# Two more features of a squared-ReLU MLP as seven half-size products: a blind prediction and its test

## The chip, the cores and the metric

The kernel runs on one core of a Trainium2 chip. The metric is the device time of one execution in microseconds (us); lower is better. Before the change the median of three runs is 1310.76 us (1310.34 to 1311.7).

## What is computed

The reference is an encoder trunk of two layers on a sequence of 512 rows of 1024 numbers: a mixer (layer 1 a gated delta rule, "GDN", layer 2 a gated linear attention, "GLA"), each followed by an MLP. The change is in the MLP, and in a constant that GLA uses.

```
def _sq_relu_mlp(h, w1, w2):
    a = jax.nn.relu(jnp.matmul(h, w1))
    return jnp.matmul(a * a, w2)
...
    x = _layernorm(DEEPNORM_ALPHA * x + _sq_relu_mlp(x, mlp_w1[i], mlp_w2[i]).astype(x.dtype), ln2_g[i], ln2_b[i])
```

w1 is 1024x4096 and w2 4096x1024, in float32. A float32 product is made of three matmuls: each operand is split in a high and a low part (a cast on ScalarE, L102, and a subtraction on VectorE, L107), and high x high, high x low and low x high are added up in PSUM (`mm3`, L128 to L130).

## The kernel before, in words

An MLP (`mlp`, from L352 on) works in four groups of 1024 hidden units, eight features of 128 units each. First the features of group 0 are made. Then, group by group, the second matmul of a group (`second`) is interleaved with the first matmul of the next group (`stream`): half chunks of six and chunks of twelve 512-column matmuls for w2 (tiles pX, pY, pZ) alternate with products for w1. The last group's second matmul (`last`) stands alone.

How a feature is made. In group 0 all eight are full products (`feature`): 24 matmuls of 512 columns into one PSUM bank (tile pj), then relu and square on ScalarE (L383, L384). In the other groups two features at a time (`Pair`) are made by seven half-size products after Strassen and Winograd, each of 12 matmuls of 256 columns: 84 for two features. They are numbered 1, 2, 6, 5, 7, 3, 4 in the order in which TensorE makes them. `prepare` and `late` make the weights: a split (L102, L107) for products 1 and 2 together, sums on VectorE (L464), half a split for product 5 (L470, L471), a split for 6 and 4, and one for 7 and 3. `x_blocks` makes the combinations of x once per MLP (L433 to L442) and splits them.

Three accumulators of 256 columns take the products: X (1, 6, 7, 4), Z (2) and Y (5, 3). A PSUM bank holds two. X has a bank of its own (tile fx), Z and Y share one (fyz). Between products the accumulators are read: X by ScalarE after product 1 (L499) and after 6 (L506), Z by VectorE after 2 (L503), Y by ScalarE after 5 (L509), X by VectorE after 7 (L513), Y after 3 (L517), X by ScalarE after 4 (L523, then L524). In the stream products 1 and 2 follow each other without a chunk between them; so do 6 and 5, and 7 and 3. A pair ahead has its weights made while the pair before it is multiplied.

What sets the order. A scheduler orders each engine's instructions; within `in_order(PE)` TensorE keeps the order in which the code is written. VectorE, ScalarE and GpSimd each work through their own list in order. Buffers: three for raw weights (wst), three for split weights (wh and wl), eight for raw w2 (w2r), two PSUM banks for the first matmul's products (tag pj). Each group also adds quarters of w2 to each other by accumulating transfers that GpSimd issues (L415).

`sel_masks` (L785) makes eight masks of 128x128 for GLA on GpSimd, by memsets, affine selects, subtractions and casts (L792 to L805); they are called in the first MLP through `extra`, and stand in GpSimd's list ahead of the first accumulating transfer.

Of the kernel before, what the change touches and what calls it, by code (L numbers as in the profile page):

```python
# [8 lines left out]
F32 = mybir.dt.float32  # L9
# [342 lines left out]
def mlp(c, w1, w2, g, b, out=None, extra=None, room=0):  # L352
# [14 lines left out]
    with c.banks(pj=2, X=2, Y=2, Z=2), tc.tile_pool(name="mlp", bufs=2) as pool:  # L367
# [82 lines left out]
        class Pair:  # L450
# [10 lines left out]
            def prepare(self):  # L461

                (t0, t1), h = self.t, KT // 2
                plus = lambda a, b: V.tensor_tensor(a, a, b, ALU.add)  # L464
# [26 lines left out]
            def products(self, h):  # L491

                f = 2 * self.p
                h0, h1 = [h[f // HF][:, (f + j) % HF, :] for j in range(2)]
                l, r = slice(0, HT), slice(HT, S)
                x, yz = c.bank([P, 2, HT], F32, name="fx", tag="pj"), c.bank([P, 2, HT], F32, name="fyz", tag="pj")
                X, Z, Y = x[:, 0, :], yz[:, 0, :], yz[:, 1, :]
                self.mm(X, 1)
                A.copy(h0[:, l], X)  # L499
                yield  # L500
                self.mm(Z, 2)
                with tc.high_priority(offset=200):
                    V.tensor_tensor(h0[:, l], h0[:, l], Z, ALU.add)  # L503
# [19 lines left out]
                A.activation(h0[:, r], X, AF.Relu)  # L523
                A.activation(h0, h0, AF.Square)  # L524
                yield
# [4 lines left out]
        def pair(src, where="ah"):  # L530
            return c.split(src, [P, HF, HT], pool=ring(where))
# [9 lines left out]
        def quarters(h):  # L541
            return [h[j][:, :, HT * i:HT * i + HT] for i in range(2) for j in range(2)]
# [155 lines left out]
                full(2 + j, 0, X[j])  # L698
            return norm, second_normed

        todo = [(gi, p) for gi in range(1, G) for p in range(GF // 2)]
        ready = {}

        def begin(i):

            if i < len(todo):
                ready[i] = Pair(*todo[i])
# [14 lines left out]
            act(ps, h[0][:, f, :])  # L722
        xa = {}
        xb = x_blocks(xa)
        for f in range(4, GF):
            feature(0, f, h)
            if f >= 5:
                next(xb)
            if f == 4:
                load(0, 0, 0)  # L730
            if f == 5:
                load(0, 0, 1)
            if f == 6:
                load(0, 1, 1)
                with tc.issue_after(c.last_hi.ins), tc.issue_after(c.last_lo.ins):
                    split(1)
                a = pair(quarters(h)[0])
        begin(0)
        prepare(0)
        finish(0)  # L740
        if extra:
            extra(lambda: pool.tile([P, P], F32, name="tmp", tag="tmp", bufs=2))
        def stream(gi, nh):

            for p in range(GF // 2):
                i = (gi - 1) * (GF // 2) + p
                for n, _ in enumerate(ready[i].products(nh)):
                    if n == 0:
                        begin(i + 1)
                    elif n == 1:  # L750
                        ready[i].late(1, (7, 3))
                    elif n == 3:
                        prepare(i + 1)
                    elif n == 5:
                        finish(i + 1)
                    if p == 3 and n == 2 and gi + 1 == G:
                        load(gi, 1, 0, c.wst)
                    if p == 3 and n == 2:
                        split(1, None if gi + 1 < G else True)
                        stream.a = pair(quarters(nh)[0])  # L760
                    yield

        for gi in range(G - 1):
            nh = new_h()
            more = stream(gi + 1, nh)
            n, k = 28, 0
            m = 24 if gi + 2 == G else 28
            with c.in_order(mybir.EngineType.PE):
                for i, _ in enumerate(second(gi, h, a)):
                    upto = n if i + 1 == m else min(i + 2, 7 * (i // 7) + 7) if i % 7 in (0, 2, 4, 6) else k  # L770
                    while k < upto:
                        next(more, None)
                        k += 1
                for _ in more:
                    pass
            h, a = nh, stream.a
        with c.in_order(mybir.EngineType.PE):
            norm, normed = last(G - 1, h, a)
# [5 lines left out]

def sel_masks(c, pool, tmp):  # L785

    nc = c.nc
    out = {}
    prev = None
    for w in (1, 2, 4, 8, 16, 32, 64, 128):  # L790
        f = tmp().rearrange("p (a b) -> p a b", b=w)
        nc.gpsimd.memset(f, 1.0)  # L792
        if w < P:
            nc.gpsimd.affine_select(out=f, in_=f, compare_op=ALU.is_ge, fill=0.0, base=0,
                                    pattern=[[-w, P // w], [0, w]], channel_multiplier=1)
            nc.gpsimd.affine_select(out=f, in_=f, compare_op=ALU.is_ge, fill=0.0, base=w - 1,
                                    pattern=[[w, P // w], [0, w]], channel_multiplier=-1)
        fl = f.rearrange("p a b -> p (a b)")
        if w != 2:
            m = pool.tile([P, P], mybir.dt.uint8, name=f"mu{w}", tag=f"mu{w}", bufs=1)  # L800
            if w == 1:
                nc.gpsimd.tensor_copy(m, fl)
            else:
                nc.gpsimd.tensor_tensor(prev, fl, prev, ALU.subtract)
                nc.gpsimd.tensor_copy(m, prev)  # L805
            out[w // 2] = m
        prev = fl
    return out


# [1103 lines left out]
```

## Time and profile before

| | |
|---|---|
| median of three runs | 1310.76 us |
| the profiled execution, its own time | 1311.28 us |
| its span, first to last instruction | 1309.6 us |
| mean granted TensorE clock | 0.997 |
| TensorE busy | 98% |
| VectorE busy | 84% |
| ScalarE busy | 61% |
| GpSimd busy | 10% |

The time of the profiled execution holds 1.7 us more than its span. In rows of the trace PE is TensorE, DVE VectorE, ACT ScalarE, POOL GpSimd and SP the engine that issues most transfers. A row of the timeline gives start and duration in us, engine, line, operation, out<-in, shapes and count; in square brackets stands how long the engine idled before it and who released it. A row of a group gives count | busy us, mean ns | idle before. Lines are those of the kernel before (below L805 the changed kernel's lines are one lower).

### The profile page before, as it was taken

The numbers are of one execution on the slowest core, as the hardware profiler recorded it, in microseconds if no ns is written. First come the engines' busy times: TensorE is split into PE (matmuls) and PEld (weight loads), VectorE is DVE, ScalarE is ACT, GpSimd is POOL, SyncE is SP. The second block draws the span as 40 slices with busy tenths as digits, with TensorE's granted clock in tenths as the row PEclk, the third lists the DMA queues.
The fourth block names the chain that finished last, engine by engine and source line by source line (L and its number), as shares of the span: only waits on it lengthen the run. The fifth ranks groups of instructions, "written<-read, shape, count | busy, mean of one in ns | idle before, by whom it ended". The sixth has DMA issues, their size and how long they took to land.

```text
span 1309.6 us, 22228 instructions
## 1 busy us (share of the span) xinstructions
PE 1289.4 (98%) x8586; PEld 1106.3 (84%) x8586; DVE 1106.3 (84%) x1795; ACT 804.8 (61%) x1604; POOL 134.6 (10%) x190
## 2 busy tenths in 40 slices
PE   8999999999999999999999999999999999999996
PEld 6778888788878899999998888888888899999985
DVE  7888888988868998999989697877888789989987
ACT  5767676677543656666657754564456566666656
POOL 5000000000003710101102100000000001101021
PEclk9999999999999999999999999999999999999998
DMA  5333313233332664576647521211316376556565
GB/s 191 99 106 96 98 55 108 81 114 96 114 110 84 175 172 169 119 203 161 177 145 154 140 97 56 74 62 52 103 59 218 87 210 165 142 176 139 171 143 144
DMA packets 47805, 165.92 MB, mean 127 GB/s; under 512 B 5923, under 2 KB 6611, under 8 KB 47699
## 3 DMA queue, kind: packets, MB, share of 16 engines
q1 hardware_dynamic: 33603, 114.52, 25.8%
q0 software_dynamic: 13984, 49.95, 18.7%
q8 instruction: 67, 1.10, 0.3%
q14 instruction: 39, 0.32, 0.1%
q10 hardware_dynamic: 112, 0.03, 0.0%
HBM read 125.00 MB, written 2.65 MB: 97 GB/s over the span
## 4 chain that ended last, share of the span: by engine, by line
PE 91%; ACT 3%; DVE 3%; issue 1%; DMA 1%; SPq 0%; DVEq 0%; ACTq 0%
PE pjv L128 3%; PE pjv L129 3%; PE pjv L130 3%; PE pX L130 3%; PE pX L129 3%; PE fx L130 3%; PE fx L128 3%; PE fx L129 3%; PE pX L128 3%; PE m L1776 3%; PE fyz L128 3%; PE fyz L130 3%; PE fyz L129 3%; PE pY L129 2%; PE pY L130 2%; PE pY L128 2%
## 5 line engine op out<-in xcount | busy, mean ns | idle before, releaser
L102 ACT CAST wh<-wst 128x1024 fp32r<-128x1024 f32 x151 | 158.5, 1050 | 104.8 <-PE fyz L129 28.2
L107 DVE TENSOR_TENSOR wl<-wst,wh 128x1024 fp32r<-128x1024 f32 x149 | 183.2, 1232 | 40.3 <-ACT wh L102 40.2
L107 DVE TENSOR_TENSOR w2l<-w2r,w2h 128x1024 fp32r<-128x1024 f32 x92 | 111.5, 1222 | 21.6 <-ACT w2h L102 21.6
L102 ACT CAST w2h<-w2r 128x1024 fp32r<-128x1024 f32 x94 | 98.4, 1048 | 42.5 <-DMA w2r<-w2r 22.8
L415 POOL DMA_DIRECT2D w2r<-w2r x56 | 47.9, 887 | 492.9 <-DVE w2l L107 388.0
L464 DVE TENSOR_TENSOR wst<-wst 128x512 f32<-128x512 f32 x120 | 80.0, 687 | 0.8
L102 ACT CAST ah<-h 128x1024 fp32r<-128x1024 f32 x56 | 58.8, 1050 | 30.6 <-PE pY L129 12.0
L107 DVE TENSOR_TENSOR al<-h,ah 128x1024 fp32r<-128x1024 f32 x56 | 68.4, 1221 | 6.6 <-ACT ah L102 6.6
L130 PE MATMUL pX<-w2h,al 128*128 128x512 f32 x168 | 66.3, 394 | 0.0
L129 PE MATMUL pX<-w2l,ah 128*128 128x512 f32 x168 | 65.9, 392 | 0.0
L128 PE MATMUL pX<-w2h,ah 128*128 128x512 f32 x168 | 65.5, 390 | 0.0
L128 PE MATMUL pjv<-wh,xth 128*128 128x512 f32 x128 | 54.7, 428 | 0.0
L130 PE MATMUL fyz<-xh,wl 128*128 128x256 f32 x192 | 53.5, 278 | 0.0
L130 PE MATMUL fx<-xth,wl 128*128 128x256 f32 x192 | 53.4, 278 | 0.0
L128 PE MATMUL fyz<-xh,wh 128*128 128x256 f32 x192 | 53.4, 278 | 0.0
L128 PE MATMUL fx<-xth,wh 128*128 128x256 f32 x192 | 53.2, 277 | 0.0
L130 PE MATMUL fx<-xh,wl 128*128 128x256 f32 x192 | 53.2, 277 | 0.0
L129 PE MATMUL fx<-xtl,wh 128*128 128x256 f32 x192 | 53.2, 277 | 0.0
L129 PE MATMUL fyz<-xl,wh 128*128 128x256 f32 x192 | 53.1, 277 | 0.0
L129 PE MATMUL fx<-xl,wh 128*128 128x256 f32 x192 | 53.1, 277 | 0.0
L128 PE MATMUL fx<-xh,wh 128*128 128x256 f32 x192 | 53.1, 277 | 0.0
L129 PE MATMUL pj<-xtl,wh 128*128 128x256 f32 (+1 forms) x160 | 52.0, 326 | 0.2 <-DVE xtl L194 0.2
(542 smaller groups left out, 4312.7 us busy)
## 6 DMA issues: line engine op xcount, KB each, us to landing
wst<-in_w SPq DMA_DIRECT2D x68, 512.0 KB, 4.6
w2r<-in_w SPq DMA_DIRECT2D x60, 512.0 KB, 4.6
w2r<-w2r POOLq DMA_DIRECT2D x56, 512.0 KB, 5.7
wst<-in_a_in SPq DMA_DIRECT2D x31, 512.0 KB, 4.1
wst<-in_b_vr SPq DMA_DIRECT2D x16, 512.0 KB, 3.3
wst<-in_a_out SPq DMA_DIRECT2D x8, 512.0 KB, 4.6
wst<-in_b_in SPq DMA_DIRECT2D x8, 512.0 KB, 3.4
wst<-in_b_out SPq DMA_DIRECT2D x8, 512.0 KB, 3.2
```

The lines of the kernel that those rows point to most:

```text
L102: h = nc.scalar.copy(hi, src)
L107: self.halves = h, nc.vector.tensor_tensor(lo, src, hi.bitcast(F32), ALU.subtract)
L128: mm(ps, ah, bh, start=start, stop=False, **kw)
L129: mm(ps, ah, bl, start=False, stop=False, **kw)
L130: self.last_mm = mm(ps, al, bh, start=False, stop=stop, **kw)
L415: nc.gpsimd.dma_start(blocks[a + (q,)], blocks[b + (q,)], accum_op=ALU.add)
L464: plus = lambda a, b: V.tensor_tensor(a, a, b, ALU.add)
L1776: T.matmul(ps[:, d, :], *ops(d), start=True, stop=True)
```

## The change

Features 6 and 7 of group 0 ("features 7 and 8" counted from one) become a pair of seven products, ahead of the stream and with no chunks between them. For this x is combined one feature earlier, the pair's weights are made during features 4 and 5, and the split of the first w2 block stands later. Z moves from Y's bank into X's: the tiles are now fxz (X and Z) and fy. The masks are made by iota on GpSimd and comparisons on VectorE, and are called after the first group's second matmul. One `in_order(PE)` spans all that follows feature 5.

```
-                x, yz = c.bank([P, 2, HT], F32, name="fx", tag="pj"), c.bank([P, 2, HT], F32, name="fyz", tag="pj")
-                X, Z, Y = x[:, 0, :], yz[:, 0, :], yz[:, 1, :]
+                xz, y = c.bank([P, 2, HT], F32, name="fxz", tag="pj"), c.bank([P, 2, HT], F32, name="fy", tag="pj")
+                X, Z, Y = xz[:, 0, :], xz[:, 1, :], y[:, 0, :]
                 self.mm(X, 1)
                 A.copy(h0[:, l], X)
                 yield
-                self.mm(Z, 2)
+                self.mm(Z, 2, False)
                 with tc.high_priority(offset=200):
                     V.tensor_tensor(h0[:, l], h0[:, l], Z, ALU.add)
                 yield
                 self.mm(X, 6, False)
...
-                self.mm(Y, 5, False)
+                self.mm(Y, 5)
...
-        todo = [(gi, p) for gi in range(1, G) for p in range(GF // 2)]
+        todo = [(0, GF // 2 - 1)] + [(gi, p) for gi in range(1, G) for p in range(GF // 2)]
...
-        for f in range(4, GF):
+        for f in (4, 5):
             feature(0, f, h)
+            next(xb)
+            load(0, 0, f - 4)
...
         begin(0)
+        next(xb)
         prepare(0)
         finish(0)
+        load(0, 1, 1)
+        with tc.issue_after(c.last_hi.ins), tc.issue_after(c.last_lo.ins):
+            split(1)
+        a = pair(quarters(h)[0])
+        whole = contextlib.ExitStack()
+        whole.enter_context(c.in_order(mybir.EngineType.PE))
+        for n, _ in enumerate(ready[0].products(h)):
+            step(0, n)
...
+            if extra and gi == 0:
+                with tc.issue_after(c.halves[1].ins):
+                    extra(lambda: pool.tile([P, P], F32, name="tmp", tag="tmp", bufs=2))
...
+    for k in range(n):
+        w = 1 << k
+        f = tmp()
+        G.iota(f.rearrange("p (a b) -> p a b", b=w), pattern=[[1, P // w], [0, w]], base=0, channel_multiplier=0,
+               allow_small_or_imprecise_dtypes=True)
+        m = out[w if k else 0] = pool.tile([P, P], mybir.dt.uint8, name=f"mu{w}", tag=f"mu{w}", bufs=1)
+        V.tensor_scalar(m, f, pf[:, k:k + 1], None, ALU.not_equal if k else ALU.is_equal)
```

`step(i, n)` is the old body of the stream's loop: after product n of pair i it starts, prepares or finishes pair i + 1.

How it moves instructions, at three places. First TensorE, in the first MLP, where product 1 of the stream's second pair ends and product 2 begins (wh_6233 and wl_6234 are the split weights of both; what stands in brackets is the engine that the matmul waits for). Before:

```order
L128 MATMUL fx_6344<-xth_5398,wh_6233 128x256
L129 MATMUL fx_6344<-xtl_5399,wh_6233 128x256
L130 MATMUL fx_6344<-xth_5398,wl_6234 128x256
L128 MATMUL fyz_6345<-xth_5398,wh_6233 128x256 [waits Activation_49]
L129 MATMUL fyz_6345<-xtl_5399,wh_6233 128x256
L130 MATMUL fyz_6345<-xth_5398,wl_6234 128x256
```

The wait before is for the pair before it: its last read of the bank that fyz now takes (L523). The same place now:

```order
L128 MATMUL fxz_6344<-xth_5398,wh_6233 128x256
L129 MATMUL fxz_6344<-xtl_5399,wh_6233 128x256
L130 MATMUL fxz_6344<-xth_5398,wl_6234 128x256
L128 MATMUL fxz_6344<-xth_5398,wh_6233 128x256 [waits Activation_49]
L129 MATMUL fxz_6344<-xtl_5399,wh_6233 128x256
L130 MATMUL fxz_6344<-xth_5398,wl_6234 128x256
```

Product 2 now writes the tile of product 1, and the count that it waits for is the one that the copy L499 of this pair's product 1 raises. TensorE's order is otherwise that of before, apart from features 6 and 7.

Second ScalarE, in the first MLP, from the relu of feature 6 to the first pair of the stream, before (wh and w2h are casts of w1 and w2, ah one of the hidden units):

```order
L383 ACTIVATE h<-pj 128x512
L384 ACTIVATE h<-h 128x512
L102 CAST wh<-wst 128x1024
L383 ACTIVATE h<-pj 128x512
L384 ACTIVATE h<-h 128x512
L102 CAST ah<-h 128x1024
L499 COPY h<-fx 128x256
L102 CAST wh<-wst 128x1024
```

Now, from the relu of feature 5, over the pair ahead of the stream, to the first pair in it:

```order
L383 ACTIVATE h<-pj 128x512
L102 CAST wh<-wst 128x1024
L384 ACTIVATE h<-h 128x512
L499 COPY h<-fxz 128x256
L102 CAST wh<-wst 128x1024
L522 ACTIVATE h<-h 128x256
L506 COPY h<-fxz 128x256
L102 CAST wh<-wst 128x1024
L509 COPY h<-fy 128x256
L470 CAST wh<-wst 128x512
L518 ACTIVATE h<-h 128x512
L519 ACTIVATE h<-h 128x512
```

The first copy L499 stands behind a cast of weights for product 6, which waits for VectorE's sums. After these rows come L523, L524, two casts and the L499 of the stream's first pair.

Third VectorE, in the first MLP, behind the splits of x: before, the weights of the stream's first pair and then the first sums of hidden units.

```order
L464 TENSOR_TENSOR wst<-wst 128x512 x4
L107 TENSOR_TENSOR w2l<-w2r,w2h 128x1024
L471 TENSOR_TENSOR wl<-wst,wh 128x512
L464 TENSOR_TENSOR wst<-wst 128x512
L107 TENSOR_TENSOR wl<-wst,wh 128x1024
L577 TENSOR_TENSOR h<-h 128x4x256
```

Now the weights of the pair ahead of the stream, and the add of its product 2 (L503):

```order
L464 TENSOR_TENSOR wst<-wst 128x512
L107 TENSOR_TENSOR w2l<-w2r,w2h 128x1024
L464 TENSOR_TENSOR wst<-wst 128x512 x2
L471 TENSOR_TENSOR wl<-wst,wh 128x512
L464 TENSOR_TENSOR wst<-wst 128x512 x2
L107 TENSOR_TENSOR w2l<-w2r,w2h 128x1024
L107 TENSOR_TENSOR al<-h,ah 128x1024
L107 TENSOR_TENSOR wl<-wst,wh 128x1024
L107 TENSOR_TENSOR w2l<-w2r,w2h 128x1024
L503 TENSOR_TENSOR h<-h,fxz 128x256
```

Four wide operations, splits of w2, of hidden units and of weights, stand between the sums and the add that product 6 waits for.

More of the change, by code (lines that the diff above doesn't have):

```diff
@@ L724, in mlp, with step @@
         xb = x_blocks(xa)
-        for f in range(4, GF):
-            feature(0, f, h)
[L727 to L737, printed above, removed]
+        def step(i, n):
+            if n == 0:
+                begin(i + 1)
+            elif n == 1:
+                ready[i].late(1, (7, 3))
+            elif n == 3:
+                prepare(i + 1)
+            elif n == 5:
+                finish(i + 1)
+        for f in (4, 5):
+            feature(0, f, h)
+            next(xb)
+            load(0, 0, f - 4)
         begin(0)
+        next(xb)
         prepare(0)
         finish(0)
-        if extra:
-            extra(lambda: pool.tile([P, P], F32, name="tmp", tag="tmp", bufs=2))
+        load(0, 1, 1)
[6 more added lines that the diff above has]
+            step(0, n)
         def stream(gi, nh):
             for p in range(GF // 2):
-                i = (gi - 1) * (GF // 2) + p
+                i = (gi - 1) * (GF // 2) + p + 1
                 for n, _ in enumerate(ready[i].products(nh)):
[L748 to L755, printed above, removed]
+                    step(i, n)
                     if p == 3 and n == 2 and gi + 1 == G:
@@ L767, in mlp @@
             m = 24 if gi + 2 == G else 28
[L768 to L775, printed above, removed]
-            h, a = nh, stream.a
-        with c.in_order(mybir.EngineType.PE):
-            norm, normed = last(G - 1, h, a)
+            for i, _ in enumerate(second(gi, h, a)):
+                upto = n if i + 1 == m else min(i + 2, 7 * (i // 7) + 7) if i % 7 in (0, 2, 4, 6) else k
+                while k < upto:
+                    next(more, None)
+                    k += 1
+            for _ in more:
+                pass
+            h, a = nh, stream.a
+            if extra and gi == 0:
+                with tc.issue_after(c.halves[1].ins):
+                    extra(lambda: pool.tile([P, P], F32, name="tmp", tag="tmp", bufs=2))
+        norm, normed = last(G - 1, h, a)
+        whole.close()
         with contextlib.nullcontext() if out is not None else tc.issue_after(normed[1].ins):
```

28 lines of the change are left out of this document (8 added, 20 removed).

## The prediction

> **What bounds the kernel now.** I read the page first: span, engines, chain of waits.
>
> ```profile
> span 1309.6 us, 22228 instructions
> ...
> PE 1289.4 (98%) x8586; PEld 1106.3 (84%) x8586; DVE 1106.3 (84%) x1795; ACT 804.8 (61%) x1604; POOL 134.6 (10%) x190
> ...
> PE 91%; ACT 3%; DVE 3%; issue 1%; DMA 1%; SPq 0%; DVEq 0%; ACTq 0%
> ```
>
> TensorE is busy in 98% of the span and makes 91% of the chain that ended last. An average hides stages, so I then read the busy time by stretches around the places the change touches: features 4 to 7 and the start of the first stream in the first MLP, and features 6 and 7 in the second MLP (columns: length, then PE, PEld, DVE, ACT and POOL with counts, clock, DMA share, GB/s).
>
> ```profile
> 421.00:454.00 33.00, 33.00 (x194) 29.03 (x193) 31.57 (x28) 21.84 (x30) 28.29 (x31) 1.00 0.56 177
> 454.00:490.00 36.00, 36.00 (x236) 32.67 (x235) 32.17 (x39) 23.00 (x32) 5.05 (x6) 1.00 0.73 167
> 1012.00:1027.00 15.00, 15.00 (x67) 12.25 (x66) 7.09 (x9) 5.51 (x8) 1.70 (x2) 1.00 0.68 201
> ```
>
> In all three TensorE never idles, at full clock. So a matmul saved there is saved from the end, and a wait put on TensorE there is added to it. VectorE has 1.4 us to spare in the first stretch (33.00 less 31.57) and 7.9 us in the last.
>
> **Part 1: fewer matmul columns, -2.9 us.** Two full features are 48 products of 512 columns; the pair is 84 of 256. Durations of single matmuls overlap, so I take starts (start, duration, engine and line):
>
> ```profile
> 442.94 0.40 PE L128 MATMUL pj<-xth,wh 128*128 128x512 f32 x1
> 453.97 0.39 PE L128 MATMUL pX<-w2h,ah 128*128 128x512 f32 x1
> 455.36 0.28 PE L128 MATMUL fx<-xth,wh 128*128 128x256 f32 x1
> 456.72 0.28 PE L128 MATMUL fyz<-xth,wh 128*128 128x256 f32 x1
> 458.09 0.39 PE L128 MATMUL pX<-w2h,ah 128*128 128x512 f32 x1
> ```
>
> Features 6 and 7 run from 442.94 to 453.97: 11.03 us. Products 1 and 2 of a pair take 458.09 - 455.36 = 2.73, so seven take 9.56. The difference is 1.47 us per MLP, 2.9 for both. It lies wholly on TensorE, which bounds.
>
> **Part 2: product 2 behind the copy of product 1, +14.0 us in 22 pairs.** This is the costly edit. Product 2 now goes into the other half of product 1's bank. The program keeps whole banks apart, not halves: already before, product 5 waited for VectorE's read of Z, the other half of its bank. So in the built program the wait on product 2's first matmul counts up to the copy L499, which can only start when product 1 is done. Before, that copy was due at product 6, a chunk later. Nothing can be moved ahead: TensorE's order is fixed, and the next matmuls stand behind the waiting one.
>
> The size, from the second pair, where ScalarE came straight from L524 to the copy, and from the last pair:
>
> ```profile
> 475.91 0.28 PE L130 MATMUL fx<-xth,wl 128*128 128x256 f32 x1
> 476.02 0.28 PE L128 MATMUL fyz<-xth,wh 128*128 128x256 f32 x1
> 476.22 0.37 ACT L499 COPY h<-fx 128x256 f32<-128x256 f32 x1
> 1242.50 0.28 PE L128 MATMUL fyz<-xth,wh 128*128 128x256 f32 x1
> 1242.70 0.37 ACT L499 COPY h<-fx 128x256 f32<-128x256 f32 x1
> ```
>
> The copy ends at 476.59, 0.57 us after product 2 started, and again 0.57 after it in the last pair (1243.07 against 1242.50). It starts 0.31 us after the last matmul's start. An idle ScalarE does no better: in the third pair the copy followed a wait for TensorE.
>
> ```profile
> 495.26 0.28 PE L130 MATMUL fx<-xth,wl 128*128 128x256 f32 x1
> 495.57 0.38 ACT L499 COPY h<-fx 128x256 f32<-128x256 f32 x1 [0.47 <-PE fx L130]
> 363.77 0.76 ACT L1717 CAST Dd<-lv 64x256 f16<-64x256 f32 x2
> 364.58 0.22 PE L1728 MATMUL nw<-Dd,ath 128*128 128x128 f16 x1 [0.23 <-ACT Dd L1717]
> ```
>
> Waking TensorE costs 0.05 us: L1717 ends at 364.53 and the matmul that waited starts at 364.58. So a pair loses 0.57 + 0.05 = 0.62 us. At the first pair of a later group a cast stands just ahead of the copy:
>
> ```profile
> 534.02 0.28 PE L128 MATMUL fyz<-xth,wh 128*128 128x256 f32 x1
> 534.34 0.36 ACT L499 COPY h<-fx 128x256 f32<-128x256 f32 x1
> 457.19 0.37 ACT L499 COPY h<-fx 128x256 f32<-128x256 f32 x1
> ```
>
> There the copy ends 0.68 us late, so 0.73. There are 24 stream pairs; the first of each MLP is costed below. Of the other 22, 18 at 0.62 and 4 at 0.73 make 14.1; I write 14.0. Ends: 0.62 for all, 13.6; and the latest copy of the trace (457.56 against 456.72, 0.84) with 0.05 for all, 19.6.
>
> On the bank: the Trainium skill, PSUM — Partial Sum Buffer, section "PSUM bank collisions raise a hardware error", says that two engines on one bank collide even at disjoint columns, and that the chip itself does not make one wait. No run here shows a collision. By its first half the program must wait as it does; by its second half alone, without the program's wait, this part would cost nothing and the sum would be about -2.9 us (the first rival).
>
> **Part 3: the pair ahead of the stream, +5.3 us.** Seven products in a row have no chunks between them to hide ScalarE's and VectorE's steps. In the first MLP VectorE is also behind. Its pace, from the rows of both MLPs in the same work (the group of L107 and what follows):
>
> ```profile
> 421.94 3.92 DVE L433 TENSOR_TENSOR w2r<-xth,xtl 128x1024 f32<-128x1024 f32 x3
> 440.89 1.48 DVE L107 TENSOR_TENSOR wl<-wst,wh 128x1024 fp32r<-128x1024 f32 x1
> 991.19 3.49 DVE L433 TENSOR_TENSOR w2r<-xth,xtl 128x1024 f32<-128x1024 f32 x3
> 994.60 1.22 DVE L107 TENSOR_TENSOR w2l<-w2r,w2h 128x1024 fp32r<-128x1024 f32 x1
> L464 DVE TENSOR_TENSOR wst<-wst 128x512 f32<-128x512 f32 x120 | 80.0, 687 | 0.8
> ```
>
> From 421.94 fifteen wide operations took 18.95 us, 1.26 each, while GpSimd made masks (28.29 us of 33). Without it they stand 3.41 / 3 = 1.14 apart, and the 0.687 us L464 0.61. The masks leave this stretch, so I take 1.14. Fifteen wide ones (up to the split of the last combination of x) end at 439.0; then six of 0.61 and one of 1.14 stand ahead of product 6's weights: 443.8. ScalarE follows, with these rows (the cast in the page's group, 1.05):
>
> ```profile
> L102 ACT CAST wh<-wst 128x1024 fp32r<-128x1024 f32 x151 | 158.5, 1050 | 104.8 <-PE fyz L129 28.2
> 443.86 0.59 ACT L383 ACTIVATE h<-pj 128x512 f32<-128x512 f32 x1
> 444.48 0.64 ACT L384 ACTIVATE h<-h 128x512 f32<-128x512 f32 x1
> L503 DVE TENSOR_TENSOR h<-h,fyz x24: 410/421/423, 459.7 to 1244.1; 128x256 f32<-128x256 f32 x24
> ```
>
> Cast, L384 and the copy (1.05 + 0.64 + 0.37, 0.1 less at each hand-over) end near 445.7, or 446.0 if feature 5's L383 comes late; product 1 is done at 442.94 + 1.37 = 444.31. Product 2 waits 1.7. It ends at 447.4, while VectorE has four wide operations after 443.8 and then the add L503: 448.4 + 0.42 + 0.05 = 448.9. So product 6 waits 1.5 more: 3.2 together. At 1.26 per wide operation the same chain ends at 451.6, which is 5.9 late. I take 3.4, near the lower end. The Trainium skill, SBUF — State Buffer, section "Who interferes with whom", says that a VectorE operation with two SBUF inputs contends only with GpSimd instructions that read SBUF; by it the iotas that remain would not slow VectorE, and the sum would use 3.2.
>
> In the second MLP VectorE has time, and ScalarE alone counts: from feature 5's end the cast of product 6's weights (0.2 after it, when its buffer comes free), L383, L384 and the copy end 2.55 later, 2.6 with the waking, against product 1's 1.37: 1.2. Then product 6 waits for the add of product 2: 0.31 + 0.42 + 0.05 less one matmul spacing of 0.11 = 0.7. Together 1.9. Sum 3.4 + 1.9 = 5.3; ends 5.1 and 8.8.
>
> **Part 4: the first pair of each stream, +2.4 us.** Its copy now stands behind L523, L524 and two casts.
>
> ```profile
> 474.26 0.37 ACT L523 ACTIVATE h<-fx 128x256 f32<-128x256 f32 x1
> 475.53 0.63 ACT L524 ACTIVATE h<-h 128x512 f32<-128x512 f32 x1
> ```
>
> From product 4's end: 0.2 + 0.37 + 0.63 + 1.05 + 1.05 + 0.37, less overlaps of 0.3, is 3.4, while TensorE has half a chunk (453.97 to 455.36, 1.39) and product 1, 2.75 together. That is 0.7; if VectorE's sums (seven small operations, 4.0 us from product 4's start) release the second cast late, 1.3 to 1.7. I take 1.2 each.
>
> **Part 5: product 6 behind one more wide operation, +1.0 us.** In five groups the second pair's L503 now stands behind a w2l split that waits for a transfer.
>
> ```profile
> 478.27 1.05 ACT L102 CAST w2h<-w2r 128x1024 fp32r<-128x1024 f32 x1 [1.68 <-DMA w2r<-w2r]
> 479.36 1.23 DVE L107 TENSOR_TENSOR w2l<-w2r,w2h 128x1024 fp32r<-128x1024 f32 x1 [1.23 <-ACT w2h L102]
> 480.18 0.28 PE L128 MATMUL fx<-xh,wh 128*128 128x256 f32 x1
> ```
>
> The split ends at 480.59, L503 and waking at 481.0; product 6, 0.62 later than before, wants 480.8. So 0.2 each; 0.8 if the transfer moves with TensorE.
>
> **Part 6: masks, 0.** VectorE gains six shifts and a cast on a few columns and seven compares of 128x128, once, between the second group's first steps. By the nearest rows, 0.15 us (128x1, below) to 0.42 (128x256, L503), they take 2 to 6 us; I take 3, since most are small. Cover: TensorE now waits 0.62 us in each pair, which VectorE does not need. The trace before has no iota. GpSimd's last five stand ahead of the 13th accumulating transfer, which had waited long for VectorE:
>
> ```profile
> 409.73 0.15 DVE L205 SCALAR_TENSOR_TENSOR rst<-bmv,rst 128x1 f32<-128x1 f32 x1
> L796 POOL TENSOR_SCALAR_AFFINE_SELECT tmp<-tmp 128x128 f32<-128x128 f32 x7 | 7.9, 1134 | 0.3
> 551.17 1.72 POOL L415 DMA_DIRECT2D w2r<-w2r  x2 [14.39 <-DVE w2l L107]
> ```
>
> Five instructions of at most the mean affine select that they replace, 1.13 us, fit in 14.39. Without that cover w2l would come up to 6 us late.
>
> **Sum.** -2.9 + 14.0 + 5.3 + 2.4 + 1.0 = +19.8 us. On the profiled execution's 1311.28 us (span 1309.6, 1.7 outside) that is 1331.1; it lay 0.5 above the median 1310.76, so the median becomes 1330.6: **1331**.
>
> **Rivals.** (a) Faster: the wait on product 2 is for an older ScalarE step, because halves of a bank are told apart. Then only part 1 and a rest of part 3 (VectorE's lateness at product 6, 0 to 1.6 us) stay: 1308 to 1310. For it: product 2 waited on ScalarE before, too, at no cost. Against: the wait of product 5 on Z's read, and the count in the built program. It decides if the copy is not what releases product 2. Chance 0.03. (b) Dearer: ScalarE and VectorE run late in all pairs, 0.89 instead of 0.62 (+5.5), part 5 at 0.8 (+3): 1339 to 1342. For it: 61% and 84% busy engines whose casts stand ahead of the copy; against: TensorE's waits give them time. Chance 0.17. (c) Cheaper: the pair ahead of the stream hides what part 3 charges beyond 0.62 for the copy, as does part 4: -2.9 + 26 x 0.62 = +13.2, 1324. For it: VectorE's order could have slack from transfers landing early; against: 1.4 us of slack for 6 us of added work. Chance 0.1. The forecast has 0.7.
>
> Range 1324 to 1342. A measurement here can tell 0.2%, 2.6 us. Slower comes from the forecast, (b) and (c), 0.97; (a) splits 0.02 faster and 0.01 same.
>
> **What would show it.** In the profile after: waits of TensorE on ScalarE's copy L499 in all 26 pairs, near 0.6 us between the starts that part 2 shows; TensorE idle for some 43 us of the span instead of 20.2 (1309.6 less 1289.4); 84 matmuls near 9.56 us plus waits where 11.03 stood; wide VectorE operations at 1.22 in the first MLP. No wait of TensorE on L499 would make the forecast wrong, and so would waits past 1 us in every pair.

## The result, and the profile after

The changed kernel takes 1344.88 us (median of 5, 1343.05 to 1345.49) against 1311.62 for the kernel before (5 runs): ratio 1.0252, 95% interval 1.0237 to 1.0267. That is +33.3 us; +19.8 was forecast, and the range ended at 1342.

The page of the changed kernel: span, engines, the chain that ended last, and the group of the matmuls that wait.

```profile
span 1342.7 us, 22380 instructions
...
PE 1303.5 (97%) x8658; PEld 1113.5 (83%) x8658; DVE 1117.2 (83%) x1829; ACT 811.5 (60%) x1616; POOL 109.4 (8%) x163
...
PE 78%; DVE 9%; ACT 8%; issue 3%; DMA 2%; SPq 0%; DVEq 0%; ACTq 0%; POOLq 0%
...
L128 PE MATMUL fxz<-xth,wh 128*128 128x256 f32 x312 | 89.6, 287 | 15.3 <-ACT h L499 15.3
```

Two things are to be seen. TensorE is now idle for 1342.7 - 1303.5 = 39.2 us instead of 20.2, and the waits on L499 stand in the chain. But its busy time also grew, from 1289.4 to 1303.5, although it has fewer columns to multiply. Part of this growth belongs to the waits: of the 0.63 us that one costs, the trace counts 0.46 as idle, and the slow restart behind it counts as busy (both below), some 8 us for 29 waits. The rest, and the columns saved, are left over. So there is a second cost, and the prediction had only the first.

The first, as forecast: the copy L499 in the view by line (under it, the matmuls that waited for it: us, times), and the second pair of the first MLP in the timeline.

```profile
L499 ACT COPY h<-fxz x26: 352/372/372, 446.7 to 1273.8; 128x256 f32<-128x256 f32 x26
...
  PE fxz L128: 15.3, 26
```

```profile
481.25 0.28 PE L130 MATMUL fxz<-xth,wl 128*128 128x256 f32 x1
481.57 0.37 ACT L499 COPY h<-fxz 128x256 f32<-128x256 f32 x1
481.99 0.38 PE L128 MATMUL fxz<-xth,wh 128*128 128x256 f32 x1 [0.46 <-ACT h L499]
482.21 0.28 PE L129 MATMUL fxz<-xtl,wh 128*128 128x256 f32 x1
482.33 0.28 PE L130 MATMUL fxz<-xth,wl 128*128 128x256 f32 x1
```

All 26 pairs wait. From the last matmul of product 1 to the first of product 2 is 0.74 us where 0.11 was usual: 0.63 lost, forecast 0.62. What the prediction left out stands one row below: after a wait the second matmul starts 0.22 us behind the first, not 0.11. Each wait on the copy costs TensorE 0.11 more to get going again.

The second cost is in the spacing of matmuls that wait for nothing. First the changed kernel, by the first matmuls of a chunk, of product 6 behind it and of product 5. Then the kernel before: the end of its product 6 (which starts at 480.18, quoted in the prediction), and the chunk between products 5 and 7.

```profile
483.46 0.40 PE L128 MATMUL pY<-w2h,ah 128*128 128x512 f32 x1
486.26 0.28 PE L128 MATMUL fxz<-xh,wh 128*128 128x256 f32 x1
487.68 0.28 PE L128 MATMUL fy<-xh,wh 128*128 128x256 f32 x1
```

```profile
481.54 0.28 PE L128 MATMUL fyz<-xh,wh 128*128 128x256 f32 x1
482.91 0.39 PE L128 MATMUL pY<-w2h,ah 128*128 128x512 f32 x1
485.68 0.28 PE L128 MATMUL fx<-xh,wh 128*128 128x256 f32 x1
```

A chunk of twelve takes 2.80 us instead of 2.77, and product 6 takes 1.42 instead of 1.36, at the same clock. All matmuls in the product are slower to much the same degree, near 0.119 apart instead of 0.113.

Both MLPs, added up from the starts of all their matmuls: the waits with the restarts behind them, and by how much the spacings of half products exceed 0.1133 us each, and those of chunks 0.2308, added up. Each cell has the first MLP, then the second, in us; the kernels are those of the experiments below.

| kernel | median us | waits and restarts | half products | chunks |
|---|---|---|---|---|
| before | 1311.6 | 0.6, 0.2 | 1.6, 1.6 | -0.3, -0.4 |
| after | 1344.9 | 13.6, 13.0 | 4.7, 1.5 | 1.7, 1.7 |
| before_bank | 1332.8 | 11.9, 10.1 | 2.0, 2.0 | -0.4, -0.4 |
| after_bank_back | 1320.3 | 3.2, 0.9 | 4.9, 1.3 | 1.6, 1.7 |
| after_place | 1343.0 | 13.9, 12.6 | 2.7, 3.3 | 1.2, 1.5 |
| before_shift64 | 1313.7 | 0.5, 0.2 | 4.5, 1.7 | -0.6, -0.4 |
| before_w2_60 | 1317.1 | 0.5, 0.2 | 2.6, 2.8 | 1.6, 1.6 |
| after_place256 | 1337.3 | 14.3, 13.5 | 2.1, 1.3 | -0.4, 0.0 |
| after_best | 1315.8 | 4.9, 1.1 | 1.0, 0.7 | 0.0, 0.0 |
| before_stride | 1312.1 | 0.5, 0.2 | 0.6, 0.6 | 0.0, 0.0 |
| before_masks | 1315.1 | 1.9, 0.2 | 4.5, 1.7 | -0.6, -0.4 |
| best_oldmasks | 1317.9 | 6.2, 1.3 | 0.9, 0.6 | 0.0, 0.0 |
| before_pair2 | 1312.1 | 0.6, 1.3 | 1.5, 2.2 | -0.2, 0.0 |

For the changed kernel that is +25.8 of waits and restarts, +3.0 of half products, +4.0 of chunks (before rounding), and -2.9 for the columns saved: 29.9 in the MLPs. The rest, some 3 us, lies outside the MLPs. About 1.2 stand ahead of the first MLP (its features start at 421.66 instead of 420.43), and go with a lower granted clock in the first 50 us of the profiled execution, 0.97 instead of 1.00 (last but two in the row). Of the kernels below, only the profile of before_masks shows 0.97 there too, and its features start 2.2 us late. The row of the changed kernel, then that of the kernel before:

```profile
0.00:50.00 50.00, 46.27 (x208) 36.31 (x209) 36.72 (x86) 29.32 (x62) 18.27 (x46) 0.97 0.51 170
```

```profile
0.00:50.00 50.00, 46.30 (x215) 36.24 (x216) 38.25 (x88) 30.53 (x66) 18.18 (x46) 1.00 0.55 181
```

What changed for the spacing is where tiles lie. Of a matmul's two operands in SBUF, the moving one streams through (x, or a split of w2), and the weights are loaded ahead (wh, or ah and al). The built programs give the byte at which each tile starts in a partition; this is the moving operand's start less the weights', modulo 256:

| | before | after, first MLP | after, second MLP |
|---|---|---|---|
| combinations of x (products 6, 5, 7, 3) less wh, by wh buffer | 0xc0, 0x40, 0xc0 | 0x00, 0x80, 0x00 | 0xc0, 0x40, 0xc0 |
| w2h, w2l less ah, al | 0x00 | 0x60 | 0x60 |

Two edits did this, neither of them about placement. The new masks bring two small tiles of 28 bytes each (pi, pf); each takes 32, and what follows in the first MLP moves by 64. And since x is combined earlier, its tiles and a padding of 96 bytes (0x60) ahead of them are allotted before w2h and w2l instead of after them.

### The profile page after: what moved, and what is told of

It is laid out like the page before. It is cut to its first block, busy times and chain, and to the rows that moved or that the text cites. A ratio compares the mean times of both kernels' runs of the same rounds, so it can differ in the third digit from the quotient of the medians.

```text
span 1342.7 us, 22380 instructions
## 1 busy us (share of the span) xinstructions
PE 1303.5 (97%) x8658; PEld 1113.5 (83%) x8658; DVE 1117.2 (83%) x1829; ACT 811.5 (60%) x1616; POOL 109.4 (8%) x163
## 4 chain that ended last, share of the span: by engine, by line
PE 78%; DVE 9%; ACT 8%; issue 3%; DMA 2%; SPq 0%; DVEq 0%; ACTq 0%; POOLq 0%
PE fxz L128 4%; PE fxz L129 4%; PE fxz L130 3%; PE pjv L128 3%; PE pjv L129 3%; PE pjv L130 3%; PE pX L129 3%; PE pX L128 3%; PE pX L130 3%; PE m L1775 3%; ACT wh L102 2%; PE scp L1007 2%; PE pY L129 2%; PE pY L128 2%; PE pY L130 2%
## 5 line engine op out<-in xcount | busy, mean ns | idle before, releaser
L107 DVE TENSOR_TENSOR wl<-wst,wh 128x1024 fp32r<-128x1024 f32 x151 | 185.3, 1229 | 48.5 <-ACT wh L102 47.8
L107 DVE TENSOR_TENSOR w2l<-w2r,w2h 128x1024 fp32r<-128x1024 f32 x92 | 111.4, 1223 | 16.6 <-ACT w2h L102 16.6
L128 PE MATMUL fxz<-xth,wh 128*128 128x256 f32 x312 | 89.6, 287 | 15.3 <-ACT h L499 15.3
L130 PE MATMUL fxz<-xth,wl 128*128 128x256 f32 x312 | 86.9, 278 | 0.0
L129 PE MATMUL fxz<-xtl,wh 128*128 128x256 f32 x312 | 86.7, 278 | 0.0
L128 PEld LDWEIGHTS fxz<-xth,wh 128*128 128x128 f32 x312 | 58.6, 188 | 22.7 <-ACT h L499 20.5
L107 DVE TENSOR_TENSOR al<-h,ah 128x1024 fp32r<-128x1024 f32 x56 | 68.5, 1223 | 7.2 <-ACT ah L102 7.2
L128 PE MATMUL pX<-w2h,ah 128*128 128x512 f32 x168 | 66.3, 395 | 0.0
L128 PE MATMUL fxz<-xh,wh 128*128 128x256 f32 x208 | 58.8, 283 | 2.1 <-DVE h L503 2.1
L129 PEld LDWEIGHTS fxz<-xtl,wh 128*128 128x128 f32 x312 | 58.7, 188 | 2.1
L130 PEld LDWEIGHTS fxz<-xth,wl 128*128 128x128 f32 x312 | 58.7, 188 | 0.0
L128 PE MATMUL fy<-xh,wh 128*128 128x256 f32 x208 | 58.5, 281 | 0.0
L129 PE MATMUL fxz<-xl,wh 128*128 128x256 f32 x208 | 58.3, 280 | 0.0
L130 PE MATMUL fy<-xh,wl 128*128 128x256 f32 x208 | 58.2, 280 | 0.0
```

What stands on the lines that cost most here:

```text
L107: self.halves = h, nc.vector.tensor_tensor(lo, src, hi.bitcast(F32), ALU.subtract)
L128: mm(ps, ah, bh, start=start, stop=False, **kw)
L129: mm(ps, ah, bl, start=False, stop=False, **kw)
L130: self.last_mm = mm(ps, al, bh, start=False, stop=stop, **kw)
```

## The experiments

The theory from the profile: waits on the copy with their restarts, and placement. Rivals: the waits come with the seven products in a row; the wider spacing follows from the stalls, or from other traffic.

**before_bank: the bank alone.**

```
...
-                X, Z, Y = x[:, 0, :], yz[:, 0, :], yz[:, 1, :]
+                X, Z, Y = xz[:, 0, :], xz[:, 1, :], y[:, 0, :]
...
-                self.mm(Z, 2)
+                self.mm(Z, 2, False)
...
-                self.mm(Y, 5, False)
+                self.mm(Y, 5)
```

> The kernel before with one edit: Z in X's bank, Y alone in the other. Theory (the wait is on the copy, and each wait costs TensorE a refill besides): 24 waits of 0.62 to 0.72 us on L499, the two pairs that lead a stream 1.0, each followed by a second matmul that starts 0.22 instead of 0.11 us after the first: 24 x 0.75 + 0.6 = +18.6 us on the kernel before, 1330. As predicted (0.62 a pair, no refill): +15.5, 1327. Rival (the bank is not the cause, the waits come from the seven products in a row): within 2.6 us of the kernel before. The spacing of half-size matmuls and chunks stays as before (no tile of SBUF moves).

1332.83 against 1311.04 for the kernel before, ratio 1.0163 (1.0149 to 1.0177): +21.8. The line of the copy in this kernel:

```profile
L499 ACT COPY h<-fxz x24: 359/372/373, 456.4 to 1262.8; 128x256 f32<-128x256 f32 x24
...
  PE fxz L128: 12.0, 24
```

So the edit of the banks alone, four lines, brings two thirds of the loss: 24 waits that cost 0.62 to 1.08 us each, 16.0 together, restarts 2.8, and 2.1 of product 6 waiting for the add L503. That is 3.2 more than the 18.6 expected: the waits of product 6 were not in it, and spacing adds 0.8. Product 2 runs 0.118 apart in pairs where it ran 0.113, with its tiles in SBUF where they were. So placement alone doesn't set the spacing; here product 2 starts behind a wait.

**after_bank_back: everything but the bank.**

```
-                X, Z, Y = xz[:, 0, :], xz[:, 1, :], y[:, 0, :]
+                X, Z, Y = x[:, 0, :], yz[:, 0, :], yz[:, 1, :]
...
```

> The changed kernel with the banks of before: X alone, Z and Y together. Theory: the 26 waits on L499 and their refills go (19.6 waited, 3.0 refill), some of the lateness at the pair ahead of the stream comes back as a wait of product 6 on VectorE's add or on its weights (0 to 3 us): 1344.9 - 22.6 + 0 to 3 = 1322 to 1325, still 11 to 14 above the kernel before, because matmuls of the first MLP's products stay 0.118 to 0.120 apart and w2l matmuls 0.237. Rival (the wider spacing is a consequence of the stalls): spacing returns to 0.113 and 0.230 with them, 1315 to 1318.

1320.26, ratio to before 1.0069 (1.0055 to 1.0082): 24.6 less than the changed kernel, and 2 below the range expected. The waits on the copy went, and the spacing stayed as wide as it was (4.9, 1.3; 1.6, 1.7). So the wider spacing does not follow from the waits on the copy.

**after_place: a first try at the tiles.**

```
...
-                room=32, extra=lambda tmp: gc.append(GlaConst(c, gp, a["b_gate_b"][0], a["b_norm_g"][0], tmp)))
+                room=96, extra=lambda tmp: gc.append(GlaConst(c, gp, a["b_gate_b"][0], a["b_norm_g"][0], tmp)))
...
                 xa[i] = c.split(f, [P, KT // 2, HT], pool=(pool, f"xh{i}", f"xl{i}", 1))
+            gap(32)
```

> The changed kernel with two paddings in SBUF and nothing else: 64 bytes more ahead of the first MLP's tiles (room 32 to 96), 32 bytes behind the combinations of x, so that x, ah and the splits of w2 lie at the same remainders of 128 bytes as before. Theory (the spacing of matmuls hangs on where weights and moving operands lie in a partition): half products of the first MLP back to 0.113 to 0.114 (-3.1 us), matmuls with w2l back from 0.237 to 0.229 (-2.0 us in each MLP): 1344.9 - 7.1 = 1337.8. Rival (VectorE's, ScalarE's or the transfers' traffic widens the spacing, or the instruction stream): no change, 1344 to 1346. The waits on L499 stay at 0.62.

1342.95: -1.9, not -7.1, and by the time alone (1341.55 to 1346.06) not clear of no change at all. As stated, modulo 128, the theory was wrong. The products in it showed the way: in the first MLP those on the second wh buffer (x 0xc0 ahead) went to 0.113 to 0.115 but for one, those on the other two (0x40 ahead) stayed at 0.117 to 0.120 for the most part. Buffers lie 4224 bytes apart, so that every second one differs by 128: the remainder to look at is of 256. The splits of w2 had come to 0x80, not 0.

**before_shift64: 64 bytes in the kernel before.**

```
-                room=32, extra=lambda tmp: gc.append(GlaConst(c, gp, a["b_gate_b"][0], a["b_norm_g"][0], tmp)))
+                room=96, extra=lambda tmp: gc.append(GlaConst(c, gp, a["b_gate_b"][0], a["b_norm_g"][0], tmp)))
```

> The kernel before with 64 bytes more ahead of the first MLP's tiles and nothing else, as the two small tiles of the new masks add them. Theory (placement): half products with the combinations of x (6, 5, 7, 3) of the first MLP go from 0.113 to 0.118 or 0.120, 48 products x 12 x 0.005 = +2.9 us; ah and w2 move together, so chunks stay at 0.2303; the second MLP is as before: 1314.5. Rival (no hold of placement on the spacing): within 1 us of the kernel before.

1313.72 (11 runs), ratio 1.0020 (1.0011 to 1.0029): +2.7, with half products up by 2.9 and no instruction moved. Products 6 and 5 begin, in the timeline:

```profile
479.60 0.28 PE L128 MATMUL fx<-xh,wh 128*128 128x256 f32 x1
481.04 0.28 PE L128 MATMUL fyz<-xh,wh 128*128 128x256 f32 x1
```

1.44 us for the product that took 1.36. This is the price of the masks' two small tiles.

**before_w2_60: the splits of w2 moved by 96 bytes.**

```
-            gap(96)
             for i, f in ((5, f22), (6, f11), (7, f21), (3, f12)):
...
+                    gap(96)
                     split(1)
```

> The kernel before with the 96 bytes of padding that stand between the splits of w2 and the combinations of x moved ahead of the splits of w2: w2h and w2l then lie 0x60 further from ah and al, as in the changed kernel, and nothing else moves (the padding's memset stands a little later). Theory (what counts is the distance of the moving operand from the weights, modulo 256 bytes): the chunks' spacing goes from 0.2303 to 0.2333, 660 + 671 matmuls x 0.003 = +4.0 us, half products as before: 1315. Rival (chunks became slower in the changed kernel because other traffic met them): within 1 us of the kernel before.

1317.08, ratio 1.0039 (1.0025 to 1.0053): +5.5. A chunk takes 2.81:

```profile
482.00 0.40 PE L128 MATMUL pY<-w2h,ah 128*128 128x512 f32 x1
484.81 0.28 PE L128 MATMUL fx<-xh,wh 128*128 128x256 f32 x1
```

Chunks are up by 3.8, as stated. Half products are up too, by 1.0 and 1.2, though none of them reads w2h or w2l. Those that became clearly slower stand directly behind a chunk: in every other pair products 6 and 4, and in the pairs between product 1, go from 0.113 to 0.118. Products 2 and 3, which follow another product, keep their spacing. So what TensorE multiplies just ahead, here the chunk that reads the moved tiles, is the nearest suspect; no run tested it.

**after_place256: the remainders of 256.**

```
-                room=32, extra=lambda tmp: gc.append(GlaConst(c, gp, a["b_gate_b"][0], a["b_norm_g"][0], tmp)))
+                room=224, extra=lambda tmp: gc.append(GlaConst(c, gp, a["b_gate_b"][0], a["b_norm_g"][0], tmp)))
...
                 xa[i] = c.split(f, [P, KT // 2, HT], pool=(pool, f"xh{i}", f"xl{i}", 1))
+            gap(160)
```

> The changed kernel with x, ah and the splits of w2 at the same remainders of 256 (not 128) bytes as before: 192 bytes more ahead of the first MLP's tiles, 160 behind the combinations of x. Theory (modulo 256): half products of the first MLP lose 4.7 - 1.6 = 3.1 us, chunks 2.0 in each MLP: 1344.9 - 7.1 = 1338; the waits on L499 stay. Rival (the distance is not it, since the run at remainders of 128 bytes gained 1.9): again about -2, 1343.

1337.27: -7.6, as stated; the rival's 1343 is out. Products 6 and 5 of the third pair take their old 1.36:

```profile
504.94 0.28 PE L128 MATMUL fxz<-xh,wh 128*128 128x256 f32 x1
506.30 0.28 PE L128 MATMUL fy<-xh,wh 128*128 128x256 f32 x1
```

**before_sweep: a map.**

```
-                w12 = c.split(t0, [P, KT, P], at=64)
+                w12 = c.split(t0, [P, KT, P], at=self.at)
...
+                self.at = ((0, 0, 32, 32, 64, 64, 96, 96, 128, 128, 16, 16) if out is None else (48, 48, 80, 80, 112, 112, 64, 64, 8, 8, 120, 120))[k]
```

> The kernel before with the split weights of each stream pair put 0 to 128 bytes into their tiles (another offset every two pairs) and the splits of w2 0 to 112 bytes into theirs (another for each block): its time says nothing, its spacings draw the map. Theory (distance of the moving operand from the weights, modulo 256): half products 0.113 where x lies 0xc0 ahead of wh, 0.118 to 0.120 at 0, 0x40 and 0x80, and unknown between; chunks 0.2303 at 0 and 0.2333 at 0x60 and 0x80. Rival (the three wh buffers differ in themselves): the spacing follows the buffer, not the offset in it.

It ran once, 1318.86: 7.4 above the kernel before, about what the wider spacings add up to. Spacing of the half products, by how far x lies ahead of wh modulo 256 (count, mean):

```
0x00  14  0.119     0x40  10  0.117     0x80  14  0.118     0xc0  18  0.115
0x10   5  0.119     0x50   5  0.118     0x90   9  0.118     0xd0   9  0.119
0x20   5  0.117     0x60   5  0.120     0xa0   9  0.118     0xe0   9  0.118
0x30   5  0.117     0x70   5  0.119     0xb0   9  0.118     0xf0   9  0.118
```

(Those at 0x08, 0x78, 0x88 and 0xf8 lie at 0.118 to 0.119.) 0xc0 has the lowest mean, and the same buffers are slower at other remainders, so the buffer alone does not decide. But the map is no rule. At 0xc0 single products range from 0.113 to 0.118. At 0x40 eight products ran at 0.118 and two at 0.113; both are product 5, which runs at 0.113 at 0x40 in the kernel before as well, in all 12 pairs where it lies there. The second wh buffer never came to 0xc0 in this run; the next kernel puts it there. For chunks the map shows no such single place (means of 0.229 to 0.234).

**before_stride: all three wh buffers at 0xc0.**

```
...
-        t = self.whl.tile([P, D + 32], F32R, name=name, tag=name)
+        t = self.whl.tile([P, D], F32R, name=name, tag=name)
...
-        return t[:, at // 4:at // 4 + math.prod(shape[1:])].rearrange("p (a b) -> p a b", b=shape[-1])
+        return t[:, :math.prod(shape[1:])].rearrange("p (a b) -> p a b", b=shape[-1])
```

> The kernel before with split weights in tiles of 4096 instead of 4224 bytes, all at remainder 0xc0 of 256, and 256 bytes of padding around them so that no other tile's remainder changes. Theory (modulo 256): the products that used the second wh buffer, 0.118 apart until now, go to 0.1133: 22 products in each MLP x 12 x 0.0047 = -1.2 each, and what else is above 0.1133 goes, together -2.5 to -3.2 us: 1308. Rival (the second buffer is slow for another reason): 1311.

1312.05, ratio 1.0001 (0.9992 to 1.0010): no gain, where 1308 was expected. The half products did go to 0.113 or 0.114 on all three buffers (all but four of 168), -2.1 us in all. But chunks behind slow products had been shorter (2.74), and they give 0.7 back; features, whose weights moved too, give 1.1 back.

**after_best: banks of before, and all remainders.**

```
+                room=224, extra=lambda tmp: gc.append(GlaConst(c, gp, a["b_gate_b"][0], a["b_norm_g"][0], tmp)))
...
+            gap(160)
...
+        t = self.whl.tile([P, D], F32R, name=name, tag=name)
...
+                X, Z, Y = x[:, 0, :], yz[:, 0, :], yz[:, 1, :]
```

> The changed kernel with the banks of before, the paddings of the run before this one, and split weights (wh, wl) in tiles of 4096 bytes that all start at the same remainder, so that x lies 0xc0 ahead of them for every buffer. From the run with the banks of before, 1320.3: half products 4.9 + 1.3 to about 0.2, -6.0; chunks 1.6 + 1.7 to -0.7, -4.0: 1310.3. If only the second buffer's 0.118 stays, 1313. Rival (placement is worth 2 us, as in the first try): 1318.

1315.84, ratio 1.0030 (1.0019 to 1.0041). Without the bank's waits and the placement, 4.2 of the 33 us are left. From the first feature behind the transposes of x to the last matmul of the last chunk, the second MLP now gains 1.0: 308.9 us, 309.9 before. The first loses 3.0 (309.8 against 306.8), by waits of the pair ahead and of later pairs, of which two rows are shown (this kernel's lines stand 4 lower: L111 is L107, L132 is L128, L528 is L524, and in best_oldmasks L387 is L383):

```profile
447.78 0.39 PE L134 MATMUL fx<-xh,wl 128*128 128x256 f32 x1 [0.73 <-DVE wl L111]
576.22 0.39 PE L132 MATMUL fyz<-xth,wh 128*128 128x256 f32 x1 [1.17 <-ACT h L528]
```

The expectation missed by 5.5: the spacings gained 7.8 instead of 10.0, features lost 0.6 by their weights' new places, and waits grew by 1.9 where they were to stay.

**before_masks: the masks alone.** The kernel before with the new `sel_masks` and its later call.

> The kernel before with the masks of the change alone (iota and comparisons, called after the first group's second matmul). The prediction's part 6: 0, 1311.6. Theory: the two small tiles move what follows by 64 bytes (+2.7, as measured with padding), and the wait of 1.0 us on kdt in the second mixer, which all kernels with the new masks show, comes with them: 1315. The trace between 421 and 454 shows VectorE's wide operations at 1.22 instead of 1.26 to 1.36, without gain for the time.

1315.09, ratio 1.0032 (1.0019 to 1.0044): +3.6, of which 2.9 are half products. The rest is mostly one wait of 1.12 us with its restart. It stands some 33 us behind the comparisons (L803 in this kernel), not at them:

```profile
L803 DVE TENSOR_SCALAR mu<-tmp,pf x7: 278/279/286, 539.6 to 543.6; 128x128 uint8<-128x128 f32 x7
...
577.35 0.38 PE L128 MATMUL fyz<-xth,wh 128*128 128x256 f32 x1 [1.12 <-ACT h L523]
```

Product 2 waits for ScalarE, which had waited 2.90 us for VectorE (L517) just before. The wait goes with the new masks: after_bank_back and after_best have it, the kernel before and best_oldmasks don't. By which steps the masks make VectorE late there is open. In the changed kernel no pair of that stretch waits longer than usual for the copy. The wait in the second mixer did not come: that part of the expectation is wrong, and that the total of 1315 was met is luck.

**best_oldmasks: after_best with the masks of before.**

> The best form of the change so far (banks of before, padded, 1315.8) with the masks of before at their old place behind the weights of the pair ahead. Theory: the wait on kdt in the second mixer goes (-1.0), and GpSimd's work of 28 us slows VectorE in the first MLP, where the pair ahead of the stream already waits for it (product 6, 0.9 + 0.1 us): 0 to +2.5 there, 1315 to 1317.5. Rival (the masks don't touch VectorE): 1314.8.

1317.86, 2.0 more than after_best. The intervals of their ratios to the kernel before overlap (here 1.0033 to 1.0063, there 1.0019 to 1.0041), so the time alone does not settle it; their waits differ by 1.5. Between 421 and 444 us GpSimd is busy (fifth number with a count) for 21.67 us, against 2.04 in after_best:

```profile
421.00:444.00 23.00, 23.00 (x152) 20.93 (x151) 21.68 (x19) 16.39 (x22) 21.67 (x25) 1.00 0.62 203
```

VectorE gets 19 instructions done, against 23 in after_best, and the pair ahead waits longer:

```profile
447.98 0.39 PE L132 MATMUL fyz<-xth,wh 128*128 128x256 f32 x1 [2.02 <-ACT h L387]
451.40 0.39 PE L134 MATMUL fx<-xh,wl 128*128 128x256 f32 x1 [1.13 <-DVE wl L111]
```

The wait on kdt, which was to go, stayed at 0.9 us. So moving the masks away costs time alone (before_masks), and seems to gain some only with the pair ahead of the stream.

**before_pair2: the pair ahead in the second MLP alone,** with the banks and masks of before.

> The kernel before with the pair ahead of the stream in the second MLP alone, with the banks and masks of before and the splits of w2 at their old remainder: what is left of the change where VectorE and ScalarE have time. 84 half products for two features, -1.5; waits of its first products, +0.9 as in the best form of the change; chunks at 0 instead of -0.35 of their nominal spacing, +0.3: 1311.6 - 0.3 to - 0.7 = 1311. Rival (the gain of 1.5 comes whole): 1310.1. Neither is more than 0.2%.

1312.13, ratio 1.0006 (0.9998 to 1.0015): no difference. Waits and restarts take 1.1 of the 1.5 saved, half products 0.6. No form that ran beats the kernel before.

## Why the prediction was wrong, point by point

The direction and the mechanism of the waits were right; the sum was 13.5 too small. The step that failed is one that the sum takes without a word: that every matmul that doesn't wait runs at its spacing of before, so that moving tiles, by the masks among others, costs 0. It cost 7.0 us (3.0 on half products, 4.0 on chunks). With the old remainders the changed kernel takes 1337.27 (after_place256), within the range stated. A second term was too small: 0.05 us for waking TensorE leaves out the restart, 3.3 us over 29 waits.

- **Part 1, columns, -2.9.** The count is as stated, and after_best shows a gain in the second MLP. But 9.56 us for a pair supposed matmuls 0.114 apart; its products took 1.41 to 1.44 in the first MLP. The kernel before already had both spacings: products 1 and 2 of the first stream pair, which the prediction measured, take 2.73 together, those of the second pair 2.83 (474.61 to 477.44).
- **Part 2, the copy, +14.0.** Right: the 22 waits measured 14.1 (18 at 0.62 or 0.63, 4 at 0.70 to 0.72). Undersized by the restart, 0.11 behind each wait: 22 times 0.11 is 2.5 us; 29 waits in all, 3.3. The waking was taken from a matmul's start, and the row behind it was not looked at.
- **Part 3, the pair ahead, +5.3.** 4.9: 1.59 and 1.49 in the first MLP, 1.08 and 0.75 in the second. Its two waits in the first MLP:

```profile
446.67 0.35 ACT L499 COPY h<-fxz 128x256 f32<-128x256 f32 x1
447.08 0.39 PE L128 MATMUL fxz<-xth,wh 128*128 128x256 f32 x1 [1.42 <-ACT h L499]
449.61 0.42 DVE L503 TENSOR_TENSOR h<-h,fxz 128x256 f32<-128x256 f32 x1
450.08 0.39 PE L128 MATMUL fxz<-xh,wh 128*128 128x256 f32 x1 [1.32 <-DVE h L503]
```

  The price of 1.14 per wide VectorE operation held: six of them stand between the two starts below, 6.82 us. The upper end given for this part, 8.8, does not follow from its own terms (5.9 + 1.9 = 7.8); no other number rests on it.

```profile
432.37 1.22 DVE L107 TENSOR_TENSOR xl<-w2r,xh 128x1024 fp32r<-128x1024 f32 x1
439.19 1.22 DVE L107 TENSOR_TENSOR xl<-w2r,xh 128x1024 fp32r<-128x1024 f32 x1
```

- **Part 4, first stream pairs, +2.4.** 2.8 (1.36 and 1.47).
- **Part 5, product 6 behind w2l, +1.0.** 0.4, at two places; the transfers mostly landed early enough.
- **Part 6, masks, 0.** Wrong, by what it did not look at. Time on VectorE is hidden in the changed kernel, as the prediction argued: six shifts of 0.15, a cast of 0.17 and seven comparisons of 0.28 us are 3.0 us, its own estimate.

```profile
L806 DVE TENSOR_SCALAR mu<-tmp,pf x7: 279/283/288, 545.4 to 550.0; 128x128 uint8<-128x128 f32 x7
```

  But the change of masks also moves every later tile of the first MLP by 64 bytes: +2.7 (before_shift64).
- **Not in the prediction:** the order of allotment moves w2h and w2l by 0x60, some 4 us of chunks (before_w2_60: 5.5 with the half products behind them).

The forecast terms for waits sum to 22.7 and measured 22.2; restarts add 3.3, placement 7.0, what lies outside the MLPs 3.1. Rival (a) is out, since the copy is what releases product 2, and rival (c) too, since the waits that it has hidden were there (4.9 and 2.8). Rival (b)'s time, 1339 to 1342, came nearest, by luck: the waits were not longer, which was its reason.

What stays open: 1.2 us in the second mixer, of which 1.0 is a wait of L1077 for ScalarE's kdt that the kernel before doesn't have. It comes with the pair ahead in the first MLP, whatever the masks: after_best and best_oldmasks show it, before_masks and before_pair2 don't. How the one leads to the other was not tried. About 0.7 us behind the last chunk are not explained either.

The group in the changed kernel, then in the kernel before:

```profile
L1077 PE MATMUL stp<-v,kdt 128*128 128x256 f32 x48 | 11.9, 381 | 1.0 <-ACT kdt L1067 1.0
L1078 PE MATMUL stp<-v,kdt 128*128 128x256 f32 x48 | 11.7, 379 | 0.0
```

## What to carry to other kernels

If two accumulators share a PSUM bank, ask for every matmul who last read or wrote the other half, and price the wait with the restart behind it. In a kernel whose TensorE never idles, list where the moving operands and the weights lie before and after a change: a tile of 28 bytes, or an allocation some lines earlier, can cost as much as a new wait. When busy time of TensorE rises with fewer columns to multiply, compare the spacing of the same product in both kernels.

## What was not expected of the hardware

Spacing of 256-column matmuls depends on where their operands lie in a partition. With x 0xc0 ahead of wh modulo 256 on all buffers it is 0.113 us (before_stride); at the other remainders tried, the means are 0.117 to 0.120 (before_sweep). The Trainium skill, SBUF — State Buffer, section "Who interferes with whom", says that TensorE reads moving operand and weights through two independent ports and never waits on anyone; by it placement would change nothing, and the measurement decides otherwise. But the operands' own distance is not all of it. Matmuls that read neither w2h nor w2l became slower when only these moved (before_w2_60), product 2 went from 0.113 to 0.118 on the same tiles once it stood behind a wait (before_bank), and product 5 runs at 0.113 at 0x40, where products 1, 2, 7 and 3 take 0.118 (the kernel before). A rule for this is not known.

A wait costs TensorE more than its length: the matmul behind the one that waited starts 0.22 us after it, where 0.11 is usual (29 waits of the changed kernel).
